# Matrix memory's running maxima spread to all partitions through DRAM, one tile ahead, with second buffers; stores of mixed tiles issued one step of the next tile later

## The chip, the core and the metric

The program runs on one NeuronCore of a Trainium2 chip. The metric is the device time of one execution in microseconds (us), the median of several runs; less is better. The engines are called as in the profile: PE (matrix products; PEld is its weight loads), DVE (vector), ACT (scalar), POOL (GpSimd) and SP, whose queue issues nearly all DMAs. Each engine works through its own instructions in order, and an instruction that waits holds up those behind it on its engine.

## The reference

One layer of a streaming encoder: a projection of the input, two mixers on it (a matrix memory with 4 heads of 128, and sliding window attention), an output projection with LayerNorm, and a convolutional feed-forward part. The prompt has 2048 tokens, and a batch of 8 x 16 sample tokens goes the same way. The change touches the matrix memory of the prompt. Cut to that:

```python
def step(carry, inp):
    C, n, m = carry
    qc, kc, vc, li, lf = inp
    b = jnp.cumsum(lf, axis=-1)
    inter = b + m[..., None]
    dmat = jnp.where(causal, b[..., :, None] - b[..., None, :] + li[..., None, :], -jnp.inf)
    mt = jnp.maximum(inter, jnp.max(dmat, axis=-1))
    w_inter = jnp.exp(inter - mt)
    s = jnp.einsum('bhld,bhsd->bhls', qc, kc) * jnp.exp(dmat - mt[..., None])
    num = w_inter[..., None] * jnp.einsum('bhld,bhde->bhle', qc, C) + jnp.einsum('bhls,bhse->bhle', s, vc)
    den = w_inter * jnp.einsum('bhld,bhd->bhl', qc, n) + jnp.sum(s, axis=-1)
    h = num / jnp.maximum(jnp.abs(den), jnp.exp(-mt))[..., None]
```

With M = mt - b, a running maximum over the tokens of a tile, the two exponentials are exp(a_s - M_l), where a = li - b, and exp(m - M_l).

## The kernel before

**Stages.** The prompt is cut into 16 tiles of 128 tokens. Stage I is the input projection in four blocks of tiles (`IBLOCKS`), as Strassen-like products of 128x256 matmuls (line 750, with line 775 for keys and gates). Stage O is the output projection in five blocks (`OBLOCKS`: the sample tile and 0, 1; then 2 to 5; 6 to 9; 10 to 13; 14 and 15), 128x512 matmuls of lines 225 to 227. Then come the feed-forward up (line 1897) and down (line 2101) parts. Float32 operands are split in two rounded halves, one by an ACT cast (line 220) and one by a DVE subtraction (line 221), and multiplied in three products.

**Chains.** Between the matmuls of stages I and O stand the steps of three chains, written as generators: the sample tile (`t_sample`), the matrix memory of the prompt tiles (`m_chain`) and the attention of the prompt tiles (`a_chain`). `Chains.weave` goes through the dense matmuls, adds their cost in nanoseconds to a clock of its own, and lets a chain take its next step when the wait that its last step yielded is over. A step yields its cost, the least wait until the next step, and how many of the five PSUM banks of the pool `tps` the next step needs. PE's order is this program order word for word. On the other engines a list scheduler of the framework sets the order of the same instructions from its model of their times.

**One tile of the matrix memory**, before:

- `m_rows` (lines 1114 to 1126): two PE transposes bring the tile's gate logs to four rows (`pgr`, lines 1049 and 1050); DVE scans give b, a and M (each 4x128); `hilo` (lines 1056 and 1057) writes M in two halves to `hl`; `y_row` writes -b - M beside a into `ay`; the carry `mc` is renewed. It runs once the tile before has been scaled, together with the loads of `m_load`: `qk`, `v1` and `og`.
- `m_tile`, first step: `m_rep` (line 1143) spreads -M to all 128 partitions with four matmuls, one a head, against `sel` (minus ones) into the PSUM bank `pm`. `m_cols` brings a and -b - M to columns by a transpose (line 1068), and the carried maximum of the tile before by one more matmul (line 1067, two passes on PE), into `pcol`, which DVE copies to `col`. DVE adds the causal mask to `pm` (`dt`, line 1148).
- Second step: ACT makes `wi`, exp of `pm` plus a column of `col`, one instruction a head (line 1160), and exp of `dt` (line 1154).
- Third step: scores and transposed keys on PE, then on DVE the weighted scores `sd` (line 1171) and the weighted keys `kw` (line 1240), and on POOL the weighted queries.
- Fourth step: numerators (`pnum`) and the new state on PE. Then follow the head norm and its scaling on DVE and ACT, four transposes (`pht`, line 1218), and four ACT copies into `mixm` (line 1221), which is a tile of the same single buffer as `kw`.

**Stores of mixed tiles.** `mix_out` (line 1212) sends `mixm` and the attention's `mixa` to DRAM (`zmix`) on SP's queue right behind the ACT copies that write them. `x_pair` (line 937) loads a block of `zmix` for stage O in four pieces once `chains.done` says that both mixers of its tiles are through; the load waits for the landing of the stores. In the same SP queue stand the weight loads of both stages (lines 469, 476, 479 and 502).

**Buffers.** `og` and `wi` have one buffer each, `qk` and `v1` two.

Of the kernel before, what the change touches and what calls it, by code (L numbers as in the profile page):

```python
# [14 lines left out]
P = 128  # L15
# [8 lines left out]
MH = 4  # L24
# [180 lines left out]
class Prog:  # L205
    def __init__(self, tc, a):
        self.tc, self.nc, self.a = tc, tc.nc, a

# [8 lines left out]

    def split(self, hi, lo, src):
        nc = self.nc
        nc.scalar.copy(hi, src)  # L220
        nc.vector.tensor_sub(lo, src, hi.bitcast(F32))  # L221

    def mm3(self, out, ah, al, bh, bl, start, stop):
# [3 lines left out]
        mm(out, al, bh, start=False, stop=stop)  # L227
# [74 lines left out]
    def setup(self):  # L302
# [7 lines left out]
        self.zqk = [dp.tile([8, P, P * len(b)], F32, name=f"zqk{i}") for i, b in enumerate(IBLOCKS)]  # L310
        self.zws = [[dp.tile([1 if g < KEPT else 2, P, 4, HT], F32, name=f"zws{g}_{i}") for i in range(4)] for g in range(NG)]
# [425 lines left out]
    def i_product(self, b, g, s):  # L737
# [6 lines left out]
        for c, k0 in pairs:  # L744
            m = slice(c * P, c * P + P)
            o = ps[:, c * HT:(c + 1) * HT]
            for k in (k0, k0 + 1):
                for i, (w, x) in enumerate(((wh, hh), (wh, hl), (wl, hh))):
                    l, r = (w[:, k, m], x[:, k]) if g < 2 else (x[:, k, m], w[:, k])
                    mm(o, l, r, start=s in (1, 7) and c == k == i == 0, stop=k == 3 and i == 2, skip_group_check=True)  # L750
# [311 lines left out]
    def m_cols(self, i, mp=None):  # L1062
# [8 lines left out]
        nc.vector.tensor_copy(col[:, c0:], ps[:, c0:])  # L1071
# [16 lines left out]
    def m_chain(self):  # L1088
# [3 lines left out]
        pend = None  # L1092
        for t in range(NPT):
            b, ti = self.place(t)
            while self.i_done <= b:
                yield 0, 500
            if pend is None:
                pend = self.m_load(t, b, ti), *self.m_rows(t, b, ti)
                yield 300, 7000, 2
            else:  # L1100
                yield 0, 1000, 2
            hn = self.m_norm(*(yield from self.m_tile(t, *pend)))
# [3 lines left out]
            if t + 1 < NPT and self.i_done > self.place(t + 1)[0]:  # L1106
                pend = self.m_load(t + 1, *self.place(t + 1)), *self.m_rows(t + 1, *self.place(t + 1))
            yield 300, 6800, 1
            self.m_out(t, hn[0])
            self.chains.done["m"] = t  # L1110
# [3 lines left out]
    def m_rows(self, t, b, ti):  # L1114
        V = self.nc.vector
        lf, li = self.gate_rows(self.logs_of(b), ti)
# [5 lines left out]
        self.hilo(i, M)  # L1122
        self.y_row(i, bc, M)
        mp, self.mc = self.mc, self.work("mc", [MH, 1], bufs=3)
        V.tensor_add(self.mc, bc[:, P - 1:P], M[:, P - 1:P])
        return i, mp

    def m_load(self, t, b, ti):
# [6 lines left out]
        og = self.work("og", [P, MH, P])  # L1135
# [20 lines left out]
    def m_inter(self, pm, col):  # L1156

        wi = self.work("wi", [P, MH, P])
        for h in range(MH):
            self.nc.scalar.activation(wi[:, h], pm[:, h], AF.Exp, bias=col[:, h:h + 1])  # L1160
        return wi
# [1031 lines left out]
```

## Time and profile before

| | us |
|---|---|
| median of 3 runs (2309.2 to 2310.85) | 2309.79 |
| the profiled execution, whole | 2309.77 |
| its span, first to last instruction | 2308.0 |
| PE busy in the span | 2275.2 |
| stages I and O with prompt chains, 278 to 915 us of the span: PE not busy | 6.9 |

The chains of the prompt run from about 278 to 915 us of the span; up to about 640 us beside stage I, then beside stage O. A "busy" PE counts the time from the first to the last moment in which some matmul is in the array; the matmuls overlap, so what one of them costs is read from the distance between the starts of neighbours.

### The profile page before, as it was taken

How to read it: one execution, taken by the hardware profiler on the slowest of the kernel's cores; microseconds unless marked ns; L12 is line 12 of the kernel's file. 1: busy time of each engine (PE TensorE's matmuls, PEld its weight loads, DVE VectorE, ACT ScalarE, POOL GpSimd, SP SyncE). 2: the span in 40 equal slices, each digit the busy share in tenths (PEclk: the TensorE clock that was granted, in tenths of full speed). 3: DMA queues.
4: the chain of work that ended last, by engine and by line, in shares of the span. 5: the costliest groups of instructions: out<-in, count | busy, mean ns of one | idle time of the engine just before them, and what ended most of it. 6: DMA issues, size and time to landing. Idle time of an engine off the chain costs nothing.

```text
span 2308.0 us, 39905 instructions
## 1 busy us (share of the span) xinstructions
PE 2275.2 (99%) x14425; PEld 2096.7 (91%) x14425; DVE 1806.0 (78%) x3157; ACT 1305.2 (57%) x2465; POOL 228.0 (10%) x289
## 2 busy tenths in 40 slices
PE   8999999999999999999999999999999999999998
PEld 8999999999877778999999999999999988888887
DVE  8777687786689888987888667778766787796897
ACT  5453466776766565555556455556555544654753
POOL 0001001001122121200002000002000000000100
PEclk9999999999999999999999999999999999999999
DMA  8898998889976667787777899888998786756753
GB/s 276 303 316 288 303 321 313 296 301 330 303 253 220 225 209 254 274 323 281 279 270 258 281 310 322 307 305 269 333 293 261 241 286 224 241 196 224 242 188 110
DMA packets 297365, 624.98 MB, mean 271 GB/s; under 512 B 47052, under 2 KB 140240, under 8 KB 297168
## 3 DMA queue, kind: packets, MB, share of 16 engines
q1 hardware_dynamic: 296304, 619.29, 78.4%
q10 hardware_dynamic: 864, 3.15, 0.4%
q8 instruction: 114, 1.87, 0.3%
q14 instruction: 83, 0.68, 0.1%
HBM read 451.78 MB, written 170.56 MB: 270 GB/s over the span
## 4 chain that ended last, share of the span: by engine, by line
PE 71%; DVE 7%; issue 3%; ACT 2%; DMA 2%; POOL 1%; SPq 0%; DVEq 0%; POOLq 0%; ACTq 0%
PE dps L1897 19%; PE fup L1897 19%; PE dps L2101 6%; PE fht L2101 6%; PE fup L2101 5%; PE dps L750 5%; PE dps L225 2%; PE dps L227 2%; PE dps L226 2%; PE ppo L1386 1%; DVE w L221 1%; PE psc L1337 1%; PE ppt L1380 1%; PE dps L775 1%; DMA txy<-wdn 1%
## 5 line engine op out<-in xcount | busy, mean ns | idle before, releaser
L1897 PE MATMUL dps<-hh,uw 128*128 128x384 f32 (+1 forms) x1848 | 477.4, 327 | 5.3 <-DVE u L1930 2.6
L1897 PE MATMUL fup<-hh,uw 128*128 128x384 f32 (+1 forms) x1848 | 476.4, 326 | 0.0
L1945 DVE SCALAR_TENSOR_TENSOR cc<-u,cw,cc 128x768 f32<-128x768 f32 (+1 forms) x264 | 257.8, 978 | 124.4 <-ACT cc L1943 121.0
L1897 PEld LDWEIGHTS dps<-hh,uw 128*128 128x128 f32 x1848 | 329.2, 188 | 7.6 <-DVE u L1930 3.2
L1897 PEld LDWEIGHTS fup<-hh,uw 128*128 128x128 f32 x1848 | 329.3, 188 | 0.0
L1897 PE MATMUL fup<-hl,uw 128*128 128x384 f32 (+1 forms) x924 | 301.3, 326 | 1.5 <-DVE hl L221 1.5
L1897 PE MATMUL dps<-hl,uw 128*128 128x384 f32 (+1 forms) x924 | 301.0, 326 | 0.0
L750 PE MATMUL dps<-w,oh 128*128 128x256 f32 x1344 | 250.5, 282 | 3.5 <-DMA w<-zws 1.8
L750 PEld LDWEIGHTS dps<-w,oh 128*128 128x128 f32 x1344 | 209.3, 188 | 15.8 <-issue 9.6
L220 ACT CAST uw<-wraw 128x1024 fp32r<-128x1024 f32 x126 | 123.3, 981 | 173.7 <-PE dps L2101 104.2
L221 DVE TENSOR_TENSOR w<-wraw,w 128x1024 fp32r<-128x1024 f32 (+1 forms) x155 | 180.9, 1172 | 47.5 <-ACT w L220 45.4
L220 ACT CAST w<-wraw 128x1024 fp32r<-128x1024 f32 (+1 forms) x155 | 155.3, 1009 | 95.7 <-PE dps L750 44.6
L221 DVE TENSOR_TENSOR uw<-wraw,uw 128x1024 fp32r<-128x1024 f32 x126 | 142.6, 1132 | 64.0 <-ACT uw L220 63.8
L750 PE MATMUL dps<-w,ol 128*128 128x256 f32 x672 | 186.2, 277 | 0.0
L1943 ACT ACTIVATE cc<-u,cw 128x768 f32<-128x768 f32 (+1 forms) x132 | 131.9, 1000 | 94.9 <-DVE u L1939 92.1
L1897 PEld LDWEIGHTS fup<-hl,uw 128*128 128x128 f32 x924 | 173.5, 188 | 2.4 <-DVE hl L221 2.4
L1897 PEld LDWEIGHTS dps<-hl,uw 128*128 128x128 f32 x924 | 173.5, 188 | 0.0
L750 PE MATMUL dps<-oh,w 128*128 128x256 f32 x896 | 167.2, 282 | 4.8 <-ACT zev L808 1.6
L2101 PE MATMUL fup<-uw,fu 128*128 128x512 f32 x726 | 169.0, 389 | 0.0
L2101 PEld LDWEIGHTS fup<-uw,fu 128*128 128x128 f32 x726 | 136.2, 188 | 28.2
L2101 PE MATMUL dps<-uw,fu 128*128 128x512 f32 x660 | 161.0, 389 | 0.1
L750 PEld LDWEIGHTS dps<-oh,w 128*128 128x128 f32 x896 | 139.7, 188 | 11.3 <-issue 4.1
(346 smaller groups left out, 4599.4 us busy)
## 6 DMA issues: line engine op xcount, KB each, us to landing
uw<-zw SPq DMA_DIRECT2D x176, 512.0 KB, 4.9
zw<-uw SPq DMA_DIRECT2D x88, 512.0 KB, 3.0
w<-zws SPq DMA_DIRECT2D x72, 512.0 KB, 6.3
wv<-wup SPq DMA_DIRECT2D x66, 512.0 KB, 5.8
wraw<-wi SPq DMA_DIRECT2D x62, 512.0 KB, 5.2
wraw<-zt SPq DMA_DIRECT2D x60, 512.0 KB, 4.3
wraw<-wdn SPq DMA_DIRECT2D x45, 512.0 KB, 3.8
wraw<-wo SPq DMA_DIRECT2D x40, 512.0 KB, 4.8
```

Of the source, the lines that this page charges most:

```text
L220: nc.scalar.copy(hi, src)
L221: nc.vector.tensor_sub(lo, src, hi.bitcast(F32))
L225: mm(out, ah, bh, start=start, stop=False)
L226: mm(out, ah, bl, start=False, stop=False)
L227: mm(out, al, bh, start=False, stop=stop)
L750: mm(o, l, r, start=s in (1, 7) and c == k == i == 0, stop=k == 3 and i == 2, skip_group_check=True)
L775: mm(o, x, w, start=k == i == 0, stop=k == KD - 1 and i == 2, skip_group_check=True)
L1337: nc.tensor.matmul(ps[kvh][:, j, :nk], q[rs, j0 + j], k[rs, sel], start=i == 0, stop=i == 2)
L1897: mm(ps, l[:, k], r[:, k], start=s in (1, 7) and k == 0 and i == 0, stop=k == 3 and i == 2, skip_group_check=True)
L1943: S.activation(c[:, v], u[:, v, 2:2 + n], AF.Identity, bias=w[3], scale=w[2])
L1945: V.scalar_tensor_tensor(c[:, v], u[:, v, i:i + n], w[i], c[:, v], op0=ALU.mult, op1=ALU.add)
L2101: mm(ps, l[:, k, c], r[:, k], start=s in (1, 4, 7) and u == 0 and k == 0 and i == 0, stop=u == nu - 1 and k == n - 1 and i == 2, skip_grou ...
```

## The change

1. **Spreading of -M.** `m_rep` is gone from the prompt's tiles (the sample tile keeps it). `m_rows` writes -M and the carried maximum into one tile `nmrow` of 4 x 129 (two DVE instructions where `hilo` had two). `m_spread` step 0 stores it to a DRAM tile `zrow`, and step 1 loads it back with a stride of zero over partitions into `nm`, 128 x 4 x 129, in SBUF. The mask addition and `wi` read `nm`; the bias of `wi` is its column 128. The second matmul of `m_cols` goes too, and `col` has 36 columns.
2. **A tile ahead.** `m_rows` of tile t+1 is called in the first step of tile t, right behind `m_cols` of tile t; the two DMAs of the spreading follow in its third and fourth steps. Only tile 0 has them all directly ahead of its own first step. The DVE mask addition is ordered behind the copy of `col`.
3. **Second buffers** for `og`, `wi`; `nmrow` and `nm` have two each.
4. **Stores later.** `m_out` and the attention's last step only note their mixed tile. `put_out` issues the store, and sets `chains.done`, in the next tile's first step (or, behind the last tile, a step of its own). `mixa` is allocated just ahead of the copy that fills it.
5. **Behind matmuls.** `behind_pe` gives these stores and the two DMAs of the spreading a place in the schedule behind the latest dense matmul of program order (`self.mark`). It is an order for the scheduler, not a semaphore: nothing waits for that matmul at run time.
6. The costs that steps yield to the weave go down by 570 ns a tile.

```diff
+    def behind_pe(self, dma):
+        if self.mark is not None:
+            self.tc.add_manual_dep(dma.ins, self.mark.ins.name,
+                                   mybir.DependencyInfo(mybir.DependencyClass.NoSync, mybir.DependencyReason.DATA), reason="late")
...
-    def m_rows(self, t, b, ti):
+    def m_rows(self, t):
...
         V.tensor_tensor_scan(M, self.seg[:, 0], a_, self.mc, op0=ALU.add, op1=ALU.max)
-        self.hilo(i, M)
+        nm = self.work("nmrow", [MH, 129], bufs=2)
+        V.tensor_scalar_mul(nm[:, :P], M, -1.0)
+        V.tensor_copy(nm[:, P:129], self.mc)
...
+    def m_spread(self, t, step):
+        nc, z = self.nc, self.zrow[t]
+        if step == 0:
+            self.behind_pe(nc.sync.dma_start(z.rearrange("o (h m) -> (o h) m", h=MH), self.rows[t][1]))
+            return
+        self.rows[t][1] = nm = self.work("nm", [P, MH, 129], bufs=2)
+        self.behind_pe(nc.sync.dma_start(nm.rearrange("p h m -> p (h m)"), z.to_broadcast([P, MH * 129])))
...
-        og = self.work("og", [P, MH, P])
+        og = self.work("og", [P, MH, P], bufs=2)
...
-    def m_inter(self, pm, col):
+    def m_inter(self, nm):
-        wi = self.work("wi", [P, MH, P])
+        wi = self.work("wi", [P, MH, P], bufs=2)
         for h in range(MH):
-            self.nc.scalar.activation(wi[:, h], pm[:, h], AF.Exp, bias=col[:, h:h + 1])
+            self.nc.scalar.activation(wi[:, h], nm[:, h, :P], AF.Exp, bias=nm[:, h, P:129])
...
-        self.mix_out(t, 0, mix)
+        self.put["m"] = t, 0, mix
...
+    def put_out(self, c):
+        if self.put[c]:
+            self.mix_out(*self.put[c])
+            self.chains.done[c] = self.put[c][0]
+            self.put[c] = None
...
-        pm = self.m_rep(i)
-        col = self.m_cols(i, mp)
-        dt = self.m_masked(pm, self.mcau)
-        yield 600, 2800
+        col = self.m_cols(i)
+        with self.tc.issue_after(self.colcopy.ins):
+            dt = self.m_masked(nm[:, :, :P], self.mcau)
+        ahead = t + 1 < NPT and self.i_done > self.place(t + 1)[0]
+        if ahead:
+            self.m_rows(t + 1)
+        yield 330, 2800
+        self.put_out("m")
         emt = self.m_emt(col)
-        wi = self.m_inter(pm, col)
+        wi = self.m_inter(nm)
         self.m_exps(dt, col)
         yield 0, 5000, 2
+        if ahead:
+            self.m_spread(t + 1, 0)
         ps = self.m_scores(qk)
...
         yield 950, 4000, 4
+        if ahead:
+            self.m_spread(t + 1, 1)
...
-        self.mix_out(t, 4, mix)
+        self.put["a"] = t, 4, mix
```

How the order moves, at three places. First PE, in stage I, at the first step of the matrix memory's sixth prompt tile (`pm` is the spread of -M, `pcol` the columns, `ppo` the attention). Before:

```order
L750 MATMUL dps<-ol,w 128x256
L750 MATMUL dps<-oh,w 128x256
L1143 MATMUL pm<-hl_747,sel 128x128 x4
L1067 MATMUL pcol<-ident,mc 128x4
L1068 MATMUL pcol<-ident,ay_749 128x36
L1386 MATMUL ppo<-pth,kva 64x512 x2
L750 MATMUL dps<-oh,w 128x256
```

And now, with the line numbers of the changed file (`pgr` are the gate rows of the tile after):

```order
L759 MATMUL dps<-ol,w 128x256
L759 MATMUL dps<-oh,w 128x256
L1077 MATMUL pcol<-ident,ay_765 128x36
L1058 MATMUL pgr<-ident,g_4043 4x128
L1059 MATMUL pgr<-ident,g_4043 4x128
L1433 MATMUL ppo<-pth,kva 64x512 x2
L759 MATMUL dps<-oh,w 128x256
```

The four `pm` matmuls and the one of `mc` are gone. The two `pgr` transposes stood alone between dense matmuls before, late in the tile ahead; they now stand in this group. On PE the rest of the order is the same but for a few steps that move by some dense matmuls.

Second SP, in stage I, around the stores of a tile's mixers (`zmix`), among weight loads (`w<-zws`, `wraw`) and stores of stage I (`zog`). Before:

```order
L1266 DMA qa<-zqa_130 128x512
L1268 DMA kva<-zkv_147 128x256
L502 DMA w<-zws_3_87 128x1024
L1212 DMA zmix_161<-mixm 128x4x128
L502 DMA w<-zws_3_87 128x1024
L1212 DMA zmix_161<-mixa 128x4x128
L569 DMA xr<-xq 128x1024 x2
```

And now, the piece with the store of the maxima and their load:

```order
L1153 DMA zrow_76<-nmrow 4x129
L578 DMA xr<-xq 128x1024
L511 DMA w<-zws_2_106 128x1024 x2
L1311 DMA qa<-zqa_146 128x512
L1313 DMA kva<-zkv_163 128x256
L807 DMA zog_135<-zev 128x256
L807 DMA zog_136<-zev 128x256
L511 DMA w<-zws_1_105 128x1024 x2
L1156 DMA nm<-zrow_76 128x516
L807 DMA zog_133<-zev 128x256
```

Between the store of `zrow` and the load that waits for its landing stand nine other DMAs here. There is one such pair a tile, 32 DMAs more in all.

Third SP, in stage O, at the load of the mixed tiles 10 to 13 (`xraw`), which the stores of tile 13 precede. Before:

```order
L1212 DMA zmix_163<-mixm 128x4x128
L1212 DMA zmix_163<-mixa 128x4x128
L937 DMA xraw<-zmix_163 128x2x512
L1612 DMA zh_171<-ymix 128x1024
L937 DMA xraw<-zmix_163 128x2x512 x2
```

And now:

```order
L1242 DMA zmix_179<-mixm 128x4x128
L1130 DMA m_p<-mc 4x1
L946 DMA xraw<-zmix_179 128x2x512
L1242 DMA zmix_179<-mixa 128x4x128
L1662 DMA zh_187<-ymix 128x1024
L1153 DMA zrow_87<-nmrow 4x129
L946 DMA xraw<-zmix_179 128x2x512
```

The attention's store now stands behind the first of the loads, and so behind that load's wait for the store of `mixm`.

57 lines of the change are left out of this document (38 added, 19 removed).

## The prediction

> **What bounds the kernel now.** I read the profiled execution's page first, then windows by stage, then the waits of PE and of SP in the stretch of the chains.
>
> ```profile
> span 2308.0 us, 39905 instructions
> PE 2275.2 (99%) x14425; PEld 2096.7 (91%) x14425; DVE 1806.0 (78%) x3157; ACT 1305.2 (57%) x2465; POOL 228.0 (10%) x289
> ```
>
> The first row is the span, the second the busy time of each engine. PE is the bound over the whole program, with DVE at 78% as the next. Now the windows that hold the prompt's chains (start and end, length, busy time of PE, PEld, DVE, ACT and POOL with counts, granted clock, DMA share, GB/s):
>
> ```profile
> 278.00:640.00 362.00, 357.22 (x2976) 329.75 (x2975) 278.25 (x825) 251.01 (x649) 41.19 (x38) 1.00 0.91 311
> 640.00:915.00 275.00, 272.93 (x1501) 213.76 (x1500) 234.38 (x576) 164.78 (x412) 57.83 (x39) 1.00 0.68 230
> ```
>
> In the first, stage I with ten tiles of the chains, PE is idle for 362.00 - 357.22 = 4.8 us; in the second, stage O with six tiles, for 2.1 us. That is 6.9 us in 637, at a granted clock of 1.00. So what leaves PE's stream there shortens the time one for one, if what PE waits for comes as much earlier; and taking waits away can give 6.9 us at most. In the same stretch DVE is 77% and 85% busy, and DMA in stage I 91%: little room, but some.
>
> **What the change removes from PE.** Two places of PE's timeline in stage O, the first where the spread of -M stands, the second where the lone pair of gate transposes stands (start, duration, engine, line, operation, count):
>
> ```profile
> 661.04 0.39 PE L227 MATMUL dps<-w,ol 128*128 128x512 f32 x1
> 661.36 0.66 PE L1143 MATMUL pm<-hl,sel 36*128 36x128 f32 x4
> 661.94 0.38 PE L1067 MATMUL pcol<-ident,mc 4*128 4x4 f32 x2
> 662.25 0.25 PE L1068 MATMUL pcol<-ident,ay 36*128 36x36 f32 x1
> 662.43 1.08 PE L1386 MATMUL ppo<-pth,kva 128*64 128x512 f32 x4
> ...
> 649.19 0.40 PE L227 MATMUL dps<-w,ol 128*128 128x512 f32 x1
> 649.42 0.28 PE L1049 MATMUL pgr<-ident,g 128*4 128x128 f32 x1
> 649.54 0.27 PE L1050 MATMUL pgr<-ident,g 128*4 128x128 f32 x1
> 649.56 0.48 PE L225 MATMUL dps<-w,oh 128*128 128x512 f32 x1
> 649.88 0.39 PE L226 MATMUL dps<-w,oh 128*128 128x512 f32 x1
> 650.11 0.39 PE L227 MATMUL dps<-w,ol 128*128 128x512 f32 x1
> ```
>
> Durations overlap, so I price by distances of starts. The four `pm` matmuls take 661.94 - 661.36 = 0.58 us, the two passes of `mc` 662.25 - 661.94 = 0.31. Both go: 0.89 a tile. The matmul behind a switch away from the dense stream starts late too: 661.36 - 661.04 = 0.32 behind line 227, where dense neighbours stand 650.11 - 649.88 = 0.23 apart, so 0.09 more. For the pair of transposes the extra lies behind it (649.56 to 649.88 is 0.32). After the change the pair stands in the group of `pcol`, where a switch is paid anyway, so one of the two 0.09 goes; whether the group's first matmul still pays the other without `pm` I can't see: its gain lies between 0 and 0.09, taken at 0.09 because the pair's own first matmul, also a transpose, starts 0.23 behind line 227.
>
> The number of tiles, and where they stand:
>
> ```profile
> L1143 PE MATMUL pm<-hl,sel 36*128 36x128 f32 x64 | 10.5, 284 | 0.0
> L1148 DVE TENSOR_TENSOR dt<-pm,k_mcau x16: 636/682/693, 289.4 to 840.0; 128x512 f32<-128x512 f32 x16
> ```
>
> 64 matmuls, four a tile, are 16 tiles. The sum: 16 x 0.89 = 14.2; the first matmul's extra 16 x 0.09 = 1.4; the pair's extra for the 15 tiles whose rows are made in the tile ahead, 15 x 0.09 = 1.4. Together 17.0 us; without both extras 14.2. By the order, the other moved steps (the gate transposes, some dense matmuls around them) are the same matmuls in another sequence, worth nothing.
>
> **What it adds on other engines.** `hilo` had two DVE instructions on 4x128; the two for `nmrow` are one of that size and one of 4x1. ACT's `wi` now reads SBUF instead of PSUM, DVE's mask addition too; rows of the same shapes with both sides in SBUF are lines 1208 and 895:
>
> ```profile
> L1160 ACT ACTIVATE wi<-pm,col 128x128 f32<-128x128 f32 x64 | 18.5, 377 | 0.9 <-DVE dt L1148 0.9
> L1208 ACT ACTIVATE hn<-hn,ms 128x128 f32<-128x128 f32 x64 | 20.6, 391 | 46.5 <-DVE ms L1206 46.5
> L895 DVE TENSOR_TENSOR txy<-txy 128x512 f32<-128x512 f32 x11 | 7.5, 684 | 10.3 <-DMA txy<-wdn 10.3
> ```
>
> DVE stands even (two instructions for two, and 684 ns against 682 for the mask); ACT loses 64 x (391 - 377) ns = 0.9 us in all, under an ACT that is 69% and 60% busy in the two windows. Both cost the end nothing; if their cover were gone, 0.9 us.
>
> **The DMAs.** Each tile stores 2 KB and loads 264 KB. At 311 GB/s the ten loads beside stage I take 2.64 MB / 311 GB/s = 8.5 us of a transfer time that has 362 x 0.09 = 33 us free. Their latency is not in the trace of before; the nearest landings are
>
> ```profile
> k_sinkx<-sinkx SPq DMA_DIRECT2D x1, 0.5 KB, 4.0
> lnp<-ln_b SPq DMA_DIRECT2D x2, 256.0 KB, 5.3
> zmix<-mixm SPq DMA_DIRECT2D x17, 256.0 KB, 4.6
> y<-yacc SPq DMA_DIRECT2D x6, 256.0 KB, 2.0
> yacc<-zh SPq DMA_DIRECT2D x17, 512.0 KB, 8.0
> ```
>
> (last number: us to landing). I estimate 4.0 for the store and, from the broadcast `lnp`, 5.3 for the load; bounds 2 + 2 and 8 + 8. From the third step of a tile to the next tile's first, of some 36.7 us a tile ((840.0 - 289.4) / 15), there are about 25 us. Even 16 us fit, so the mask addition should not wait. Tile 0 alone has the spread directly ahead of its first step; PE's dense matmuls fill that.
>
> On SP the load of `nm` waits for the landing of `zrow`, and weight loads queue behind it. In stage I nine other DMAs stand between in the order shown, most of the 4.0 us; in stage O only one to three. Whether a held weight load shows is read from the casts that follow it and from what SP waits for:
>
> ```profile
> L220 ACT CAST w<-wraw 128x1024 fp32r<-128x1024 f32 (+1 forms) x98 | 97.2, 1000 | 30.4 <-PE dps L227 13.4 <-PE dps L750 9.7 <-DMA wraw<-wg 1.6
> SPq L1212 <- ACT mixm L1221: 15.1, 6, 5.3
> SPq L1136 <- DVE mr L1196: 11.3, 7, 2.7
> ```
>
> Of 30.4 us in which the casts had to wait, 23.1 were for PE to give a buffer back and 1.6 for a load: weights stand ready ahead of use. And SP today stops at the stores of `mixm` (15.1 us, up to 5.3 at once) and at the load of `og` (line 1136, 11.3) without PE's noticing. The late stores and the second `og` take these stops away; the waits for `zrow` put others of up to 4 us in their place. I cost the exchange at 0, between -6.9 (all idle time of PE gone) and what rival C gives.
>
> `mixm` is a tile of the buffer of `kw`. Its store moves to where `wi` is made, and must have landed before the next `kw`:
>
> ```profile
> L1154 ACT ACTIVATE dt<-dt,col x4: 417/423/424, 374.0 to 374.9; 128x128 f32<-128x128 f32 x4
> L1240 DVE TENSOR_TENSOR kw<-pkt,dt x1: 675/675/675, 384.9 to 384.9; 128x512 f32<-128x512 f32 x1
> ```
>
> Issued at about 374 and landed 4.6 later, it is there 6 us ahead: nothing. Should SP hold it 6 us longer, DVE waits, and what follows on PE comes late by the excess.
>
> **Blocks of stage O.** The late store delays `xraw`, and with it the last quarter of a block. Blocks 0 to 2 begin behind stage I or far behind their tiles. For the block of tiles 10 to 13:
>
> ```profile
> L937 SPq DMA_DIRECT2D xraw<-zmix x4: 431/434/621, 803.1 to 809.7; - x4
> 825.76 0.48 PE L225 MATMUL dps<-w,oh 128*128 128x512 f32 x1
> 826.42 1.21 DVE L942 TENSOR_TENSOR ol<-xraw,oh 128x1024 fp32r<-128x1024 f32 x1
> ```
>
> the block begins at 825.76, its last quarter is split at 826.42 + 1.21 = 827.6, and the order places its first use 32 matmuls on, at 833.25: 5.6 us of slack against a store later by one step, 3 to 5 us. For the last block, of tiles 14 and 15:
>
> ```profile
> 869.28 0.38 SPq L1212 DMA_DIRECT2D zmix<-mixa  x1
> 869.75 2.88 SPq L937 DMA_DIRECT2D xraw<-zmix  x4
> 890.46 0.69 DVE L942 TENSOR_TENSOR ol<-xraw,oh 128x512 fp32r<-128x512 f32 x1
> 891.03 0.39 PE L225 MATMUL dps<-w,oh 128*128 128x512 f32 x1
> ```
>
> the last split ends at 891.15 and PE uses it about there, so there is no slack. But 20 us lie between the issue of the loads and that split, and its place comes from DVE's order. I take 2 us lost for both blocks, between 0 and 4. So 17.0 - 2 = 15 us gained. The profiled execution's own time (2309.77, the span and 1.8 around it) is the median's 2309.79; 2309.8 - 15 gives **2295 us**.
>
> **Rivals.** *B: stage I is not PE's to give.* Freed PE time turns into waits for weights or DVE. For it: here DMA is at or near its limit in pieces,
>
> ```profile
> 500.00:550.00 50.00, 49.38 (x418) 45.61 (x416) 36.35 (x113) 33.53 (x86) 3.53 (x5) 1.00 1.01 357
> ```
>
> so the dense stream might go at the pace of the transfers. Against it: the casts wait for PE. Then only the six tiles beside stage O pay: 6 x (0.89 + 0.09) = 5.9, giving 2303.9.
>
> *C: slower, through SP's queue.* The load of `nm` stops SP for up to 4.0 us a tile, in stage O with little between; the weight loads behind it land late, and PE stands. It decides once the stop is longer than the lead of the weights, which would show as casts (line 220) idle on DMA instead of PE. If half of the 4.0 reaches PE in each tile, 16 x 2 = 32 us against the 15 gained: 2309.8 + 17 = 2327. For it: the stop is new and regular. Against it: stops of up to 7.3 us in the same queue today, 37.3 us in all at line 479 alone, leave PE 99% busy.
>
> ```profile
> SPq L479 <- DVE w L221: 37.3, 19, 7.3
> ```
>
> [...]
>
> *D: the relieved stops of SP also take PE's idle time away*: up to 6.9 us more, 2288. Against it: PE's idle rows name evictions of stage I, which the change does not touch:
>
> ```profile
> PE dps L750 <- ACT zev L808: 2.1, 2, 1.6
> ```
>
> **Chances.** The forecast 0.70 (its own range 2290 to 2300), B 0.13, C 0.11, D 0.06. The range 2288 to 2306 leaves out C and a part of the edges. A measurement tells 0.2% (4.6 us) from no change: faster takes the forecast, D and about half of B, 0.82; the same takes the other half of B and mild forms of C, 0.09; slower the rest of C, 0.09.
>
> **What would show it.** Right: PE's busy time falls by 14 to 17 us to about 2259, its idle time between 278 and 900 stays within 4 us of 6.9, the `pcol` group begins at the dense pitch, no wait of DVE for `nm`, casts still idle on PE. B: idle PE before 640 us grows by about 9. C: casts and PE waiting on `wraw` or `w`. Wrong: PE's busy time falls less than 14, a wait of `dt` for `nm`, or of `kw` for the store of `mixm`.

## The result and the profile after

The changed kernel takes 2318.73 us (median of 6 runs, 2315.53 to 2321.05); the kernel before took 2310.32 in 6 runs beside them. The ratio is 1.0032 with an interval of 1.0021 to 1.0043: slower by 8.4 us, where 15 us less were forecast. The profiled execution has a span 7.7 us longer than the one of before, while PE is busy for less. 7.2 of these 7.7 us are there when the feed-forward part begins: its first matmul of line 1897 starts at 916.0 us before, and the same one (line 1947) at 923.2 now. First the page of the changed kernel (span, then busy time of each engine), then its windows by stage with the columns of before:

```profile
span 2315.7 us, 39747 instructions
...
PE 2269.9 (98%) x14329; PEld 2088.3 (90%) x14329; DVE 1807.2 (78%) x3157; ACT 1308.0 (56%) x2465; POOL 228.7 (10%) x289
```

```profile
278.00:640.00 362.00, 346.83 (x2903) 318.84 (x2901) 275.16 (x796) 251.63 (x639) 39.99 (x37) 1.00 0.92 309
640.00:915.00 275.00, 269.88 (x1479) 209.61 (x1478) 234.64 (x601) 166.10 (x420) 56.18 (x40) 1.00 0.73 246
```

PE is idle for 15.2 us beside stage I, where it was 4.8, and for 5.1 beside stage O, where it was 2.1: 13.4 us of new idle time. The place where the spread of -M stood, in stage O, in PE's timeline (start, duration, engine, line, operation):

```profile
671.76 0.40 PE L235 MATMUL dps<-w,ol 128*128 128x512 f32 x1
672.09 0.25 PE L1077 MATMUL pcol<-ident,ay 36*128 36x36 f32 x1
672.27 0.27 PE L1058 MATMUL pgr<-ident,g 128*4 128x128 f32 x1
672.38 0.27 PE L1059 MATMUL pgr<-ident,g 128*4 128x128 f32 x1
672.58 1.08 PE L1433 MATMUL ppo<-pth,kva 128*64 128x512 f32 x4
```

From the first matmul of the group to `ppo` it is 0.49 us, and was 662.43 - 661.36 = 1.07. The pair of gate transposes that stood alone took 0.23 us (in the prediction's lines 649.88 - 649.19 = 0.69, less two dense distances of 0.23). Together that is 0.81 us a tile, 13.0 for 16 tiles, an estimate from these two places. So the matmuls did leave PE, and new waits ate as much and more. What PE waits for between 278 and 915 us (waiting line, releaser, total, times, longest), the five largest rows:

```profile
PE dps L759 <- ACT zev L825: 3.8, 3, 2.5
PE dps L784 <- DVE zev L831: 3.2, 2, 2.5
PE pcu L1301 <- DVE kw L1283: 2.9, 1, 2.9
PE dps L759 <- DVE zev L831: 1.8, 1, 1.8
PE ppo L1433 <- ACT pth L1428: 1.7, 1, 1.7
```

None of these rows names a weight or a transfer. PE waits for ACT and DVE to clear PSUM (`zev`, evictions of stage I) or to make an operand. So the question is what made these two late, and there the same view has two new rows, one on ACT and one on DVE:

```profile
ACT wi L1190 <- DMA nm<-zrow: 21.7, 8, 4.1
...
DVE kw L1283 <- DMA zmix<-mixm: 4.2, 2, 3.4
```

The first: ACT waits at `wi` for the landing of `nm`. One such place, in ACT's timeline (the bracket holds the wait ahead of the instruction):

```profile
327.10 1.28 ACT L1190 ACTIVATE wi<-nm 128x128 f32<-128x128 f32 x4 [2.64 <-DMA nm<-zrow]
328.29 1.03 ACT L228 CAST w<-wraw 128x1024 fp32r<-128x1024 f32 x1
329.69 1.28 ACT L1238 ACTIVATE hn<-hn,ms 128x128 f32<-128x128 f32 x4 [0.38 <-DVE ms L1236]
330.88 0.57 ACT L825 ACTIVATE zev<-dps 128x512 f32<-128x512 f32 x1
```

and what PE does behind it:

```profile
331.50 0.38 PE L759 MATMUL dps<-oh,w 128*128 128x256 f32 x1 [2.55 <-ACT zev L825]
```

This `wi` belongs to the second tile, whose columns stand on PE only at 341.5 us. Reading `nm` alone, it has no tie to its tile's first step any more, and the scheduler put it 14 us ahead of it on ACT, where the cast, `hn` and the eviction of the rows above stand behind it and start at 328.29 us and later.

The second row is the buffer that `mixm` shares with `kw`. SP's timeline at the border of the stages, changed kernel:

```profile
646.94 0.43 SPq L1689 DMA_DIRECT2D o_ln_b<-ln_b  x1
647.42 0.42 SPq L1242 DMA_DIRECT2D zmix<-mixm  x1
```

and the `kw` that waits for that store:

```profile
655.05 0.69 DVE L1283 TENSOR_TENSOR kw<-pkt,dt 128x512 f32<-128x512 f32 x1 [3.37 <-DMA zmix<-mixm]
```

In the kernel before, the store of the same tile, the tenth of its line, went out much earlier:

```profile
623.85 0.37 SPq L1212 DMA_DIRECT2D zmix<-mixm  x1
```

The late store came in SP's queue behind loads of stage O (`o_ln_b` and others); ahead of the first of `ln_g` and `ln_b` (line 1689) SP waits 3.9 us for the landing of a last store of stage I (`zkv`).

### The profile page after: what moved, and what is told of

It is laid out like the page before. It is cut to its first block, busy times and chain, and to the rows that moved or that the text cites. A ratio compares the mean times of both kernels' runs of the same rounds, so it can differ in the third digit from the quotient of the medians.

```text
span 2315.7 us, 39747 instructions
## 1 busy us (share of the span) xinstructions
PE 2269.9 (98%) x14329; PEld 2088.3 (90%) x14329; DVE 1807.2 (78%) x3157; ACT 1308.0 (56%) x2465; POOL 228.7 (10%) x289
## 5 line engine op out<-in xcount | busy, mean ns | idle before, releaser
L759 PEld LDWEIGHTS dps<-oh,w 128*128 128x128 f32 x896 | 139.9, 189 | 14.3 <-ACT zev L825 4.5
```

What stands on the lines that cost most here:

```text
L759: self.mark = mm(o, l, r, start=s in (1, 7) and c == k == i == 0, stop=k == 3 and i == 2, skip_group_check=True)
```

## The experiments

All medians are of 5 to 12 runs, each beside the kernel before (2310.2 to 2310.8 in the five sets). An interval of a ratio is about 0.002 wide, so 2 us of difference between two kernels is not told apart. The expectations weigh four theories against each other: W, ACT's `wi` waits for `nm` and evictions queue behind it; S, the late stores; Q, the waits of the new DMAs in SP's queue; L, the scheduler's new order of DVE and ACT.

**e1: `wi` held behind its tile's `emt`.**

```diff
-        self.nc.scalar.activation(emt, col[:, 36:40], AF.Exp)
+        self.emtins = self.nc.scalar.activation(emt, col[:, 36:40], AF.Exp)
...
-        wi = self.m_inter(nm)
+        with self.tc.issue_after(self.emtins.ins):
+            wi = self.m_inter(nm)
```

> The changed kernel, with one order added: ACT makes a tile's `wi` behind that tile's `emt`, so not before its columns are there. Theory W (in the changed kernel ACT's `wi` stands up to 15 us ahead of its tile, waits 21.7 us in all for the landing of `nm`, and evictions queue behind it): ACT's wait for `nm` goes from 21.7 us to below 2, the idle time of PE that follows such waits (2.55, 1.69, 1.08 and 0.71 us, together 6.0) goes, and the time falls by about 6 us, to 2313. Theory S (the late stores cost it): no change, 2319. Theory Q (SP's wait for `zrow` holds weight loads up): no change, 2319. Theory L (the list scheduler's new order of DVE and ACT puts evictions late, whatever the DMAs do): any shift of some us either way, with PE idle at other places.

Measured: 2316.40 us, ratio 1.0019 (1.0011 to 1.0028). ACT waits nowhere for `nm`, but the time falls by 2.3 us only, and PE is idle for 18.3 us between 278 and 920 us, at much the same places as without the edit (19.9). The wait of ACT was real and was a small part of the loss. The wait of PE that was shown above at 331.50 us is still there, with no `wi` ahead of it:

```profile
329.86 0.38 PE L759 MATMUL dps<-oh,w 128*128 128x256 f32 x1 [2.60 <-ACT zev L825]
```

ACT's timeline in e1 shows what holds this eviction now, the head norm `hn`, which waits for DVE:

```profile
328.04 1.28 ACT L1238 ACTIVATE hn<-hn,ms 128x128 f32<-128x128 f32 x4 [4.33 <-DVE ms L1236]
329.23 0.57 ACT L825 ACTIVATE zev<-dps 128x512 f32<-128x512 f32 x1
```

In the kernel before, the same eviction stands ahead of `hn` on ACT, and PE does not wait for it:

```profile
323.08 0.60 ACT L816 ACTIVATE zev<-dps 128x512 f32<-128x512 f32 x1
327.06 1.28 ACT L1208 ACTIVATE hn<-hn,ms 128x128 f32<-128x128 f32 x4 [3.38 <-DVE ms L1206]
```

So PE's longest wait for an ACT eviction comes with a changed order of two ACT instructions, as theory L has it. What made the scheduler change that order is not shown.

**e3: as e1, and `mixm` in a buffer of its own.**

```diff
-        mix = self.work("kw", [P, 4, P], name="mixm")
+        mix = self.work("mixm", [P, 4, P])
...
-        self.rows[t][1] = nm = self.work("nm", [P, MH, 129], bufs=2)
+        self.rows[t][1] = nm = self.work("nm", [P, MH, 129])
```

> As e1, and `mixm` has a buffer of its own apart from `kw` (`nm` gives one of its two up for the room). Theory W with the part of S that goes through the shared buffer: besides the 6 us, the wait of `kw` for the store of `mixm` (3.4 us on DVE, 2.85 us of idle PE at 655.9 us) goes: 2319 - 9 = 2310. Theory Q: 2319. Theory L: PE idle at other places, of about the same sum as in the changed kernel (19.9 us between 278 and 920 us).

Measured: 2311.65, ratio 1.0004 (0.9995 to 1.0013), 4.8 us below e1. The wait of `kw` is gone. The edit also leaves `nm` one buffer in place of two, so the gain is that of both together. PE is still idle for 17.2 us, which is what theory L expected.

**e4: stores at once.** The copies' stores are issued as before the change, without the order behind matmuls.

```diff
-        self.behind_pe(self.nc.sync.dma_start(self.zmix[b][k:k + 4, :, ti * P:ti * P + P].rearrange("k p m -> p k m"), mix))
+        self.nc.sync.dma_start(self.zmix[b][k:k + 4, :, ti * P:ti * P + P].rearrange("k p m -> p k m"), mix)
...
         self.put["m"] = t, 0, mix
+        if t < NPT:
+            self.put_out("m")
...
         self.put["a"] = t, 4, mix
+        self.put_out("a")
```

> The changed kernel with the stores of `mixm` and `mixa` issued right behind the copies that write them, as before the change; spread and buffers as changed. Theory S: 2319 falls by the 2.9 us of idle PE at `kw` and by up to 2 us at the blocks of stage O, to 2314 to 2316. Theory W and Q: no change, 2319. Theory L: a shift of some us either way.

Measured: 2312.39, ratio 1.0008 (0.9998 to 1.0018): 6.3 us less than the changed kernel, more than the theory's 3 to 5.

**e7: no DMAs of the spread.** `nm` is a constant tile, so the maxima are left out of what is computed.

```diff
+        self.nmk = self.work("nm", [P, MH, 129])
+        self.nc.vector.memset(self.nmk, -1.0)
...
         if step == 0:
-            self.behind_pe(nc.sync.dma_start(z.rearrange("o (h m) -> (o h) m", h=MH), self.rows[t][1]))
             return
-        self.rows[t][1] = nm = self.work("nm", [P, MH, 129], bufs=2)
-        self.behind_pe(nc.sync.dma_start(nm.rearrange("p h m -> p (h m)"), z.to_broadcast([P, MH * 129])))
+        self.rows[t][1] = self.nmk
```

> The changed kernel without the 32 DMAs of the spread: `nm` is one constant tile, set once, so the maxima are left out of what is computed; every other instruction stays. Theories W and Q together (the DMAs of the spread and the waits for them are the cost): the saving on PE comes out, about 13 us below before and 2 to 3 back for `kw`: 2299. Theory S or L: 2314 to 2319, since their causes stay.

Measured: 2309.38, ratio 0.9991 (0.9982 to 1.0000). 9.3 us come back, not the 20 that theories W and Q together asked for, and 14.1 us of PE's idle time remain with no DMA of the spread in the program. But 9.3 us is far more than the 2.3 of e1, which also takes ACT's wait for `nm` away. In e7 the late store at the border of the stages leaves SP at 639.06 us instead of 647.42, and the longest wait of `kw` for it is 2.6 us instead of 3.4; how the rest of the 9.3 us comes about is not shown.

**e8: e1 and e4 together.**

> The changed kernel with both edits that gained by themselves: `wi` behind `emt` (2316.4 alone) and the stores at once (2312.4 alone). If the two causes are separate, the gains of 2.3 and 6.3 us add up: 2318.7 - 8.6 = 2310, level with before. If what is left comes from the order of DVE and ACT (theory L), PE's idle time between 278 and 920 us stays at 14 to 18 us whatever the time.

Measured: 2310.85, ratio 1.0003 (0.9992 to 1.0013): the two gains add up, and the time is that of before. PE's idle time is 15.5 us, so the saving of 13 us is still lost somewhere.

**e9: e8 with the yields of before.**

```diff
-                yield 150, 7000, 2
+                yield 300, 7000, 2
...
-            yield 150, 6800, 1
+            yield 300, 6800, 1
...
-        yield 330, 2800
+        yield 600, 2800
```

> As e8, with the costs that the steps yield to the weave as they were before the change (600 and 300 ns in place of 330 and 150). Theory L in its form Y (a lower cost moves the chains' steps to other dense matmuls, where evictions of stage I collide with them): PE's idle time falls from about 17 us towards the 6.3 us of before, the time to about 2301. If the yields have no part in it: within 2 us of e8.

Measured: 2308.32, ratio 0.9995 (0.9986 to 1.0003): 2.5 us below e8, at the edge of what is told apart, with 14.4 us of idle. Form Y of theory L falls as the main cause.

**e10: e8 with the rows of the next tile at their old place.**

```diff
-        ahead = t + 1 < NPT and self.i_done > self.place(t + 1)[0]
+        ahead = False
```

> As e8, but the rows of the tile after are made where they were before the change (behind the scaling of the tile ahead), and both DMAs of the spread follow at once. Theory L in its form R (the seven DVE instructions of the rows, 1.9 us, and the gate transposes in a tile's first step come on top of the attention's softmax there, and evictions come late): the idle of PE near 461, 573 and 627 us (1.7, 1.1 and 1.7 us and 1.8 us at half clock) goes, a gain of 4 to 6 us, less what DVE then waits for `nm` (some 9.3 us of landings against 7.8 us to the next first step, 16 times up to 1.5 us, mostly hidden): 2304 to 2308. If the place has no part: 2310 or later.

Measured: 2310.77, ratio 1.0005 (0.9997 to 1.0014), no gain. But it mixes two things: `nm` now lands late, so that ACT's `wi` waits for it at eight tiles (11.5 us, up to 3.4) and DVE's mask addition at eight (14.3 us, up to 3.5), and PE waits 5.8 us for `sd`, where it waits 0.4 in the kernel before. It does not judge the place.

**e12: the price of the matmuls alone**, in the kernel before. A constant tile in SBUF is read in their place, so the maxima are left out of what is computed.

```diff
+        self.nmk = self.work("nm", [P, MH, P])
+        nc.vector.memset(self.nmk, -300.0)
...
-            self.nc.scalar.activation(wi[:, h], pm[:, h], AF.Exp, bias=col[:, h:h + 1])
+            self.nc.scalar.activation(wi[:, h], pm[:, h], AF.Exp, bias=col[:, 4 + h:5 + h])
...
-        pm = self.m_rep(i)
-        col = self.m_cols(i, mp)
-        dt = self.m_masked(pm, self.mcau)
+        pm = self.nmk
+        col = self.m_cols(i)
+        with self.tc.issue_after(self.colcopy.ins):
+            dt = self.m_masked(pm, self.mcau)
```

> The kernel before with the matmuls of `m_rep` and of the carried maximum left out for the prompt's tiles, and a constant tile read in their place (so the maxima are left out of the computation); no DMA is added, rows, stores, buffers, yields and the other matmuls stand as before. It prices the prediction's main term alone. If PE's time comes out one for one: 2310 - 14 to 17 = 2293 to 2296. If stage I cannot use it (rival B: evictions, weights and DVE set its pace): the six tiles beside stage O alone, 5 to 6 us, 2304 to 2305.

Measured: 2301.29, ratio 0.9963 (0.9951 to 0.9975): 9.1 us, between the two expectations. Six matmul passes a tile fewer, with nothing put in their place, give two thirds of their 14.2 us; PE's idle time grows from 6.3 to 10.3 us.

**e5: the kernel before with second buffers of `og` and `wi`.**

```diff
-        og = self.work("og", [P, MH, P])
+        og = self.work("og", [P, MH, P], bufs=2)
...
-        wi = self.work("wi", [P, MH, P])
+        wi = self.work("wi", [P, MH, P], bufs=2)
...
```

> The kernel before with second buffers for `og` and `wi` and nothing else. Theory S in its form B (the buffers themselves let loads and `wi` go to places where they stand in the way): slower by 2 us or more. If buffers only relieve SP: 2310, within 2 us.

Measured: 2309.31, ratio 0.9994 (0.9985 to 1.0003): nothing. PE's idle time is 6.3 us, as before.

**e6: the kernel before with the late stores** (`put_out`, `behind_pe` and the later `mixa`, as in the diff of the change).

> The kernel before with the stores of `mixm` and `mixa` a step of the next tile later and behind matmuls, and nothing else. From e4 (undoing them in the changed kernel gave 6.3 us): slower than before by 3 to 6 us, with `kw` waiting for the store of `mixm` on DVE for 3 us or more at one or two tiles. If the gain of e4 was only another order: within 2 us of before.

Measured: 2319.91, ratio 1.0038 (1.0025 to 1.0052). The late stores by themselves cost 9.1 us. The profiled execution's span, 2320.8 us, is 12.8 us longer than that of before, and one place carries about half of that. SP, DVE and PE there, and the window (columns as above) that holds the wait:

```profile
642.04 0.42 SPq L1222 DMA_DIRECT2D zmix<-mixm  x1
```

```profile
652.09 0.69 DVE L1258 TENSOR_TENSOR kw<-pkt,dt 128x512 f32<-128x512 f32 x1 [5.40 <-DMA zmix<-mixm]
```

```profile
652.93 1.41 PE L1274 MATMUL pcu<-v,kw 128*128 128x129 f32 x5 [4.41 <-DVE kw L1258]
```

```profile
640.00:655.00 15.00, 10.59 (x61) 9.38 (x60) 8.47 (x30) 7.40 (x23) 1.29 (x1) 0.91 0.97 324
```

`kw` waits 5.4 us for the landing, PE is idle for 4.4 of them, and its granted clock drops at the end of that: 0.91 on average in the window, and 0.83 from 650 to 660 us, by which 10 x (1 - 0.83) = up to 1.7 us more are lost, an estimate. That is some 6 of the 12.8 us; the rest of the new idle time lies in waits of up to 1.6 us. The landing itself was slow. The last number is the time from issue to landing, where the median of these stores in the kernel before is 4.6:

```profile
zmix<-mixm SPq DMA_DIRECT2D x1, 256.0 KB, 10.0
```

Without the wait `kw` would have stood at 652.09 - 5.40 = 646.69 us, and a landing of 4.6 would have come at 646.64.

**e13: e9 without the DMAs** (the edit of e7 on e9).

> As e9 (2308.3), without the 32 DMAs of the spread: `nm` is one constant tile (the maxima are left out of what is computed). Against e9 it prices the DMAs where nothing on ACT waits for `nm` any more. Theory Q (in SP's queue the DMAs put other loads off, as those of `txy` at 320.8 us in e9, nine us later than before, and DVE and ACT stand behind these): 2308.3 falls by 4 to 7 us to the level of e12, 2301 to 2304. If what is left between e9 and e12 is the place of the rows and of the gate transposes: within 2 us of 2308.

Measured: 2308.93, ratio 0.9996 (0.9987 to 1.0005), level with e9. With `wi` held and the stores at once, the 32 DMAs cost nothing that can be told, and theory Q falls for that kernel. In the changed kernel, where the stores are late, leaving them out gave 9.3 us (e7); the two prices are those of two kernels.

**e14: e13 with the rows at their old place** (the edit of e10 on e13).

> As e13 (2308.9; constant tile, no DMAs of the spread, so the maxima are left out), with the rows of the tile after made where they were before the change. Theory R (rows and gate transposes in a tile's first step are what is left between e13 and e12): the time falls to the level of e12, 2301 to 2303, and PE's idle between 278 and 920 us from 13.9 to about 10. If the place has no part: 2307 to 2310.

Measured: 2302.60, ratio 0.9968 (0.9956 to 0.9979): 6.3 us below e13. This edit moves seven DVE instructions and two transposes a tile, and removes nothing. What differs is seen in PE's timeline of e13, at three places:

```profile
354.54 0.49 PE L1296 MATMUL pnum<-v,sd 128*128 128x129 f32 x2 [1.92 <-DVE sd L1201]
...
569.55 0.39 PE L759 MATMUL dps<-w,oh 128*128 128x256 f32 x1 [2.39 <-DVE zev L831]
...
832.49 0.62 PE L1248 MATMUL pht<-ident,hn 128*128 128x128 f32 x2 [1.59 <-ACT hn L1238]
```

and in windows of e13 around them (third column from the right: granted clock):

```profile
350.00:360.00 10.00, 8.08 (x57) 7.89 (x56) 8.96 (x24) 2.34 (x7) 0.10 (x1) 0.83 0.89 326
570.00:580.00 10.00, 10.00 (x76) 10.00 (x75) 6.56 (x27) 3.61 (x9) 2.39 (x3) 0.83 0.87 293
830.00:840.00 10.00, 8.41 (x37) 4.86 (x37) 9.05 (x20) 5.56 (x18) 3.38 (x3) 0.83 0.52 188
```

where e14 has

```profile
350.00:360.00 10.00, 10.00 (x88) 9.85 (x86) 9.19 (x29) 3.94 (x9) 0.62 (x2) 1.00 0.95 336
565.00:580.00 15.00, 14.19 (x123) 13.77 (x122) 11.35 (x41) 6.96 (x18) 4.09 (x5) 1.00 0.96 344
815.00:840.00 25.00, 24.13 (x137) 17.85 (x136) 24.05 (x71) 15.18 (x42) 7.46 (x5) 1.00 0.59 195
```

With the rows early, PE is idle for 13.9 us against 11.8, and around three of the waits its granted clock reads 0.83 over 10 us: 10 x (1 - 0.83) = 1.7 us lost each time, 5.1 in all, an estimate from these windows. 2.1 + 5.1 = 7.2 against a difference of spans of 2308.3 - 2302.4 = 5.9: of the right size for these two executions. Over all runs the mean granted clocks are 0.9969 (11 runs of e13) and 0.9978 (6 of e14); that difference is worth 2.1 us of 2309, an estimate, so this execution of e13 had more drops than most.

**e19: the kernel before with the rows in the first step, nothing else.**

```diff
         dt = self.m_masked(pm, self.mcau)
+        if t + 1 < NPT and self.i_done > self.place(t + 1)[0]:
+            self.rows[t + 1] = self.m_rows(t + 1, *self.place(t + 1))
...
```

> The kernel before, with only the rows of the tile after made in a tile's first step; spread by matmuls, stores, buffers and yields as before. Theory R: slower than before by 4 to 7 us, 2314 to 2317, with PE idle in front of the `pgr` transposes and at evictions of stage I. If the place has no part: 2310, within 2 us.

Measured: 2311.92, ratio 1.0006 (0.9998 to 1.0015). By itself the place costs some 1.5 us, within the scatter, not 4 to 7. PE is idle for 6.1 us, and every window of 10 us in its chains shows a granted clock of 1.00. So the 6.3 us are the place's price in a kernel that has lost its `pm` matmuls, not a constant of the move. Why the two differ is not settled.

**e16: the rows at the end of the fourth step**, in e9.

> As e9 (2308.3; everything computed), with the rows of the tile after made at the end of a tile's fourth step, their store there and the load of `nm` behind the scaling. Theory R: the first step is relieved, 2302 to 2306, which would beat both kernels. If the place has no part, or the fourth step is as crowded as the first: 2307 to 2311.

Measured: 2321.71, ratio 1.0051 (1.0035 to 1.0066), worse by 13 us than e9. The step asks for five PSUM banks there, PE's idle time is 22.4 us, and DVE's mask addition waits for `nm` at three tiles (4.5 us). Which of these makes up the 13 us was not separated.

**e18: the carried maximum through `ay`**, in the kernel before.

```diff
-            nc.tensor.matmul(ps[:, 0:4], mp.to_broadcast([MH, P]), self.ident[:MH, :MH], start=True, stop=True)
-        nc.tensor.transpose(ps[:, 4:40], self.ay[i], self.ident[:36, :36])
+        nc.tensor.transpose(ps[:, 4:72], self.ay[i], self.ident[:68, :68])
...
+        V.tensor_copy(self.ay[i][64:68], self.mc.to_broadcast([MH, P]))
...
```

> The kernel before, with only the matmul of the carried maximum taken away: a DVE copy writes it as four more rows of `ay`, and the transpose that is there anyway brings it to columns (68 rows in place of 36). No DMA, no order changed by hand. Saved on PE: 16 x 0.31 = 5.0 us less some 0.03 a tile. By the share that came out in e12 (9.0 of 14.2 us): -3 us, 2307. If DVE's copy (0.2 us a tile) or the order eats it: within 2 us of before.

Measured: 2308.99, ratio 0.9996 (0.9987 to 1.0005): not told apart from before. PE's idle time between 278 and 920 us grows by some 3.5 us, of about 5 that were taken from its work: the same as in e12, on a smaller scale.

**e20: e9 with the rows at their old place and a later first step** (`yield 0, 3500, 2` for `yield 0, 1000, 2`, and the edit of e10).

> As e10 (everything computed, rows at their old place, `wi` held, stores at once; 2310.8), with the yields of before the change and 2500 ns more of least wait ahead of a tile's first step, so that `nm` has landed. If e10 lacked only this against e14 (2302.6): ACT's and DVE's waits for `nm` fall below 2 us together and the time to 2303 to 2305, below both kernels. If the landing still shows, or the later steps push the last tile and the blocks of stage O: 2308 or more.

Measured: 2346.27, ratio 1.0156 (1.0140 to 1.0173). The waits for `nm` are gone (0.5 us on DVE), but the tiles run later each time, and in stage O the dense matmuls run out before the chains are through:

```profile
800.00:840.00 40.00, 23.92 (x152) 17.41 (x153) 17.65 (x92) 27.39 (x87) 2.41 (x3) 0.74 0.40 130
```

PE is busy for 24 of these 40 us. The chains' own length is then the bound: 2.5 us more ahead of each tile, up to 37.5 us for the 15 tiles behind the first, cost 35.5 against e10. No version that computes everything beats the kernel before by more than its interval; the nearest are e5, e9 and e18.

## Why the prediction was wrong

The steps between the kernel before and the changed one, each by one experiment, in medians:

| step | from, to | us |
|---|---|---|
| matmuls of `m_rep` and the carried maximum away | before, e12 | 2310.4 to 2301.3: -9.1 |
| second buffers, `nmrow` and the rest of the rewriting | e12, e14 | to 2302.6: +1.3 |
| rows and gate transposes in the first step | e14, e13 | to 2308.9: +6.3 |
| the 32 DMAs, `wi` held | e13, e9 | to 2308.3: -0.6 |
| lower yields | e9, e8 | to 2310.9: +2.5 |
| `wi` free to stand early | e8, e4 | to 2312.4: +1.5 |
| late stores | e4, changed kernel | to 2318.7: +6.3 |

Steps of 2.5 us and less are within the scatter. Three stand clear of it. The sizes are those of this one path: another order of the same edits gives others, as e7 (9.3 us for the DMAs), e6 (9.1 for the late stores) and e19 (1.5 for the place of the rows) show. So the three causes are shown, and their shares of the 8.4 us are not fixed.

- **The bound, one for one.** "What leaves PE's stream there shortens the time one for one, if what PE waits for comes as much earlier." The condition failed for a third of it: e12 gives 9.1 us for 14.2. Where the dense stream came sooner, evictions and operands of DVE and ACT did not: PE's waits for evictions and for `ql` between 278 and 915 us are 7.0 us in e12 and 5.0 in the kernel before. The 6.9 us of idle time before were read as room behind PE; e12 shows that the others were close behind it.
- **Price of the matmuls.** 0.89 us a tile was right. The 2 x 0.09 for switches was not there: the first matmul of the group still starts 672.09 - 671.76 = 0.33 behind the dense one, and the pair of gate transposes takes 672.58 - 672.27 = 0.31 in the group, more than its 0.23 alone. By these places 13.0 us instead of 17.0 left PE.
- **Moved steps "worth nothing".** This is the first step that failed in kind. The moved matmuls are the same, but their DVE instructions were not counted: 1.9 us a tile in the changed kernel's trace (0.40, 0.28, 0.47, 0.21, 0.28, 0.15 and 0.13), moved into the step in which DVE also makes the mask addition and the attention's softmax (line 1387). One such place on DVE:

```profile
673.08 0.19 DVE L1080 COPY col<-pcol 128x36 f32<-128x36 f32 x1
673.18 0.68 DVE L1178 TENSOR_TENSOR dt<-nm,k_mcau 128x512 f32<-128x512 f32 x1
673.78 0.40 DVE L1139 TENSOR_TENSOR_SCAN r_b<-pgr,k_seg 4x128 f32<-4x128 f32 x1
674.22 0.28 DVE L1140 TENSOR_TENSOR ay<-pgr,r_b 4x128 f32<-4x128 f32 x1
674.53 0.47 DVE L1141 TENSOR_TENSOR_SCAN r_M<-k_seg,mc,ay 4x128 f32<-4x128 f32 x1
675.04 0.21 DVE L1143 TENSOR_SCALAR nmrow<-r_M 4x128 f32<-4x128 f32 x1
675.29 0.28 DVE L1069 SCALAR_TENSOR_TENSOR ay<-r_b,r_M 4x128 f32<-4x128 f32 x1
675.58 0.15 DVE L1147 TENSOR_TENSOR mc<-r_b,r_M 4x1 f32<-4x1 f32 x1
675.84 0.40 DVE L1387 CUSTOM_DVE_ANT_0 sc<-psc,k_mswa 128x256 f32<-128x256 f32 x1
```

  In the changed kernel without its DMAs, with `wi` held, the stores at once and the yields of before, the place costs 6.3 us (e14, e13); whether it is as much in the changed kernel itself was not measured.
- **The late stores: "nothing".** This is the second. Two terms were read at places that do not hold everywhere. From issue to `kw` the text has 10.9 us, at one tile in the middle of stage I (374 to 384.9); at the border of the stages the store left SP 23.6 us later than before the change (647.42 against 623.85), and DVE was ready for `kw` 4.3 us behind that (655.05 - 3.37 - 647.42). The landing was taken at its median, 4.6 us; there it took 7.6 (647.42 to 655.05), and 10.0 in e6. With 4.6, `kw` would have waited 0.3 us instead of 3.4. The text named this wait and gave it no price. The late stores are worth 6.3 us in the changed kernel (e4) and 9.1 in the kernel before (e6).
- **The landing of `nm`.** For the mask addition it holds: no wait of `dt` for `nm`. `wi` was not looked at. With its bias from `nm` it lost the tie to `pcol`, and stood on ACT before its data. The cost, 1.5 to 2.3 us (e8 against e4, e1), is small beside the 21.7 us that ACT waited: most of that was time ACT had to spare.
- **DVE and ACT work.** Right: `wi` from SBUF takes 392 ns against 377, the mask addition 680 against 682.

```profile
L1190 ACT ACTIVATE wi<-nm x64: 384/392/415, 291.1 to 837.4; 128x128 f32<-128x128 f32 x64
L1178 DVE TENSOR_TENSOR dt<-nm,k_mcau x16: 678/680/1772, 291.7 to 845.5; 128x512 f32<-128x512 f32 x16
```

- **SP's wait for `zrow` (rival C).** The stop itself was rightly costed at 0. SP stops for it at three tiles only:

```profile
SPq L1156 <- DMA zrow<-nmrow: 8.7, 3, 4.5
```

  and e13 against e9 shows no price. The time was slower than before, as in that rival, but PE waits for the landing of a weight at one place only, for 0.2 us. That the DMAs cost nothing holds without the late stores; in the changed kernel 9.3 us go with them (e7), of which e1 accounts for 2.3, and the rest stays open.
- **Blocks of stage O.** The 2 us taken off for late `xraw` were not there: no wait of PE in stage O is for `xraw` or its splits.
- **Rivals B and D.** B had the mechanism nearest to what happened: freed time in stage I turned into waits, mostly for evictions and operands of ACT and DVE and not for weights. It took the loss to be at most the gain. D fell: e5 gives `og` and `wi` their second buffers and nothing else, and PE's idle time stays at 6.3 us; e6 has the late stores alone and is slower.

The 7.7 us between the two spans add up like this: 13.0 were saved; 13.4 are new idle time and 1.7 a drop of the clock at 460 to 470 us. Ahead of the prompt's chains this execution is 2.4 us behind already: the ACT eviction (line 816, now 825) that starts at 269.13 us before starts at 271.51. In the other kernels' profiled executions it stands between 268.64 and 272.02, so I take that as scatter. That leaves some 3 us, for which no wait is on record; they stay open. The sign that the prediction gave, PE's busy time down by 14 to 17 us, failed too: it went down by 2275.2 - 2269.9 = 5.3.

## What to carry to other kernels

Count what a moved step issues on every engine, and look at what else the new place asks of them; where PE is 99% busy, as here, the engines that clear PSUM for it can be the next bound (9.1 us came out of the 14.2 that e12 takes away), and a place is a cost (6.3 us between e14 and e13). Read the slack of a delayed transfer, and its landing, at its worst tile, here the one where two stages meet and the queue holds other waits (landings of 7.6 and 10.0 us, against a median of 4.6), not at a typical one. Do not add up prices of single edits without a run that has them together: leaving out the 32 DMAs was worth 0 us here (e13) and 9 us (e7), by what stood beside them. When an edit takes an operand away from an instruction, ask what else tied it to its place in an order that a scheduler makes.

## What the runs showed of the hardware

Four waits of PE came with a cost beyond their length. Around idle times of 1.6 to 2.5 us (e13 at 354.5, 569.6 and 832.5 us; the changed kernel at 462.5) the granted clock reads 0.83 over 10 us, by which 1.7 us are lost each time, an estimate. In windows of half a microsecond it reads 0.50 from 463.0 to 466.0 us in the changed kernel, 0.70 in the next and 1.00 from 466.5 on. The dense matmuls are slower there: six groups of three of line 784 take 466.33 - 462.52 = 3.81 us, where one group takes 459.41 - 459.05 = 0.36 ahead of the wait, so 1.65 us more. The window of 10 us there:

```profile
460.00:470.00 10.00, 7.54 (x50) 7.49 (x50) 9.12 (x15) 9.20 (x19) 0.00 (x0) 0.83 0.89 268
```

Other waits of 2.55 and 2.85 us in the same execution of the changed kernel (331.5 and 655.9 us) had no such drop: the windows of 10 us from 320 to 340 and from 640 to 670 us read 1.00. What sets these waits apart is not shown.

Over many executions the changed kernel's granted clock is lower too. The mean granted clock over the span, averaged over runs, is 0.9981 for the kernel before (33 runs), 0.9957 for the changed one (6), and 0.9978 for e12 and e14. 0.0024 of 2315 us is 5.6 us, an estimate, since each run gives the clock to 0.001 only. How much of the 8.4 us this is stays open. Two executions of the changed kernel with clocks of 0.998 and 0.995 took 2317.53 and 2317.47 us; e6 has a mean clock of 0.9976 and is 9.1 us slower than before, and e4 has 0.9961 and is 2 us slower. So a lower granted clock and a longer time do not go together from kernel to kernel here.
